# A hybrid decoder layer's third pass: TensorE's order by hand, p turned on TensorE, silu through tanh

## The chip, the core and the metric

The kernel runs on one core of a Trainium2 chip. The metric is the device time of one execution in microseconds, the median of several runs. The core has five engines that run beside each other and meet at semaphores: TensorE (PE in the profile, with PEld for its weight loads), VectorE (DVE), ScalarE (ACT), GpSimd (POOL) and SyncE (SP), which here issues the DMA transfers. Sixteen DMA engines move the data.

## The reference

One layer (depth 1, so only the gMLP mixer is built) on x of 4096 tokens by 1024, with a cross-attention of 4 heads of 64 into a memory of 256 rows. All in f32.

```python
kv = einsum('bmd,de->bme', mem, mem_kv_w)          # mem_k, mem_v: 4 heads x 64
proj = einsum('bsd,de->bse', x, a_w_in)
u, v, q_x, gate = split_cols(proj, [768, 768, 256, 1024])
tok = chunked_spatial_gating(u, v, a_w_s, a_b_s)    # gelu, norm per 128, causal 128 x 128 mixing, times u
s = einsum('bshd,bmhd->bhsm', qh, mem_k) * 64 ** -0.5
xo = einsum('bhsm,bmhd->bshd', softmax(s), mem_v)
mixed = concatenate([tok, xo], -1) * silu(gate)
y = einsum('bse,ed->bsd', mixed, w_out)
x = layer_norm(ALPHA * x + y, ln_g, ln_b)
```

## The kernel before

Each f32 operand of a product is kept as two parts of type fp32r, hi and lo (`split`, L70: a cast on ACT, then a subtraction on DVE), and a product is three matmuls for each 128 of depth (`product`, L187: 4 x 3 = 12 matmuls, each of 128 weights columns by the width of the output). The large products use seven partial products in place of eight (`x_parts`, `w_parts`, `gemm`), with the two halves of the 1024 columns of depth as one index.

The 4096 tokens are taken in 16 blocks of 256 (`b`), and the layer in four passes over all blocks, because not all weights fit. Passes 1 and 2 (L290) compute the two halves of u, v, the attention's q and the last 256 gate columns; they leave u times the mixed v (`z1_d`), q (`q_d`) and the gate columns for the attention (`gx_d`) in DRAM, and pass 2 leaves three of the four parts of x (`x_d`). `memory` (L245) makes K (`kst`) and V (`vst`) in pass 2.

Pass 3 (L393 to L507) is the one around the change. For each block it does the following:
- `load_x` (L406) brings the parts of x, `load_z` (L470) brings z1, one block's q comes in `scores`, gx in `attend`.
- `scores` (L417): for each half of the tokens (`c`) and pair of heads (`hp`), four matmuls into one PSUM bank (L426); maximum and scaling on DVE (L430, L431), two exps with their sums on ACT (L434), reciprocal on DVE, the product of p and 1/sum on POOL (L437). DVE then turns p within 32 x 32 squares into `pts` (L228, through `transposed`).
- `weights_of` (L441): sixteen DMA transfers on SP's queue (L447) put the turned squares in place in `pr`, and one split over 2048 columns makes `pT`.
- `attend` (L450): 16 matmuls of V by pT (L460), the adding of the two halves on ACT and DVE (L465, L466), the product with silu(gx) (L467), the store to `z_d`.
- the gates (L497): four quarters (column half `j`, token half `i`), each of two products, 24 matmuls of 384 columns (L190). ACT's Silu (L503), POOL's product with z1 (L505), DVE's turn into `zt`, and at the end of the block four transfers (`scatter`, L236).

`scores` runs two blocks and `weights_of` one block ahead of the gates in the text. The order on each engine is not that of the text: a planner simulates the engines and places each engine's instructions, DMA issues on SP's queue too. Pass 3 has eight PSUM banks: five for gates (`acc2`) and three for scores and attends (`oth2`).

Pass 4 (L510) multiplies z by w_out and does the norm. Two of its seven weights are loaded during pass 3 (L490), the other five (L514) go to places that hold pass 3's gate weights, V, K and `pT`. Its raw z tiles (`raw3`) use memory of pass 3's pools.

Of the kernel before, what the change touches and what calls it, by code (L numbers as in the profile page):

```python
# [13 lines left out]
P = 128  # L14
# [21 lines left out]
def trunk_kernel(ctx, tc, xT, x, memT, w_kv, wl, wsT, bsT, ln_g, ln_b, out):  # L36
# [11 lines left out]
    def f(ap):  # L48
        return ap.bitcast(F32)
# [195 lines left out]
    def memory(pool, psum):  # L245
# [32 lines left out]
        for mh in range(2):  # L278
            for h in range(HEADS):
                e = h % 2  # L280
                split(vst[:, mh, h, e * HD:(e + 1) * HD], vst[:, mh, h, (1 - e) * HD:(2 - e) * HD],
                      pv[:, mh, h * HD:(h + 1) * HD])
# [7 lines left out]
    for g in range(2):  # L290
        with tc.tile_pool(name=f"mix{g}", bufs=1, reuse_waits="tile") as pool, \
# [8 lines left out]
            if first:  # L300
# [6 lines left out]
                                    fill=0.0, base=0, channel_multiplier=-1)  # L307
            split(wm[:, 0], wm[:, 1], wraw)
# [84 lines left out]
    with tc.tile_pool(name="turned", bufs=1, reuse_waits="tile") as turned, \  # L393
            tc.tile_pool(name="att", bufs=1, reuse_waits="tile") as pool, \
            tc.tile_pool(name="acc2", bufs=5, space=bass.MemoryType.PSUM, reuse_waits="tile") as psum, \
            tc.tile_pool(name="oth2", bufs=3, space=bass.MemoryType.PSUM, reuse_waits="tile") as psum2:
# [4 lines left out]
        qss = [arena[:, o:o + 1024].rearrange("p (h t) -> p h t", h=HEADS) for o in (12288, 13312)]  # L401

# [14 lines left out]
        def scores(b):  # L417
            qs = qss[b % 2]
            nc.sync.dma_start(f(qs), q_d[b].rearrange("h p t -> p h t"))
            pts = turned.tile([P, 32, 2, 32], F32, name="pts")  # L420
            for c in range(2):
                for hp in range(2):
                    ps = oth("sc")
                    for e in range(2):
                        for i in range(2):
                            nc.tensor.matmul(ps[:, e, :], qs[:, 2 * hp + e, c * P:(c + 1) * P], kst[:, i, 2 * hp + e, :],  # L426
                                             start=i == 0, stop=i == 1)
                    nm = pool.tile([P, 2], F32, name="nm", bufs=2)
                    sm = pool.tile([P, 2], F32, name="sm", bufs=2)
                    nc.vector.tensor_reduce(nm, ps, axis=AX.X, op=ALU.max)  # L430
                    nc.vector.tensor_scalar(nm, nm, -SCALE, None, op0=ALU.mult)  # L431
# [51 lines left out]
        for b in range(NB):  # L483
            xs = nxt
            if b + 1 < NB:
                nxt = load_x(b + 1)
# [142 lines left out]
```

## Time and profile before

| what | value |
|---|---|
| median of 3 runs | 1580.45 us (1579.23 to 1582.13) |
| the profiled execution, its time | 1580.65 us |
| its span | 1578.8 us |
| mean granted TensorE clock | 0.948 |
| TensorE busy | 1386.1 us, 88% of the span |
| DVE, ACT, POOL busy | 1110.3, 793.5, 717.3 us |
| DMA | 322.65 MB, 204 GB/s on average |

The first 765 us or so are passes 1 and 2, the third pass runs to about 1208, the fourth to the end. The clock is a share of 2.4 GHz, and 0.5 is the lower level of 1.2 GHz. A window of the trace gives the busy time of each engine in a stretch, and the granted clock and the DMA engines' share beside it. Lines of the timeline merge instructions that follow each other and are of one kind; the bracket is the idle time ahead and what ended it. Busy time says little by itself: the waits and the order of the work in one stretch say what the stretch is worth.

### The profile page before, as it was taken

The numbers are of one execution on the slowest core, as the hardware profiler recorded it, in microseconds if no ns is written. First come the engines' busy times: TensorE is split into PE (matmuls) and PEld (weight loads), VectorE is DVE, ScalarE is ACT, GpSimd is POOL, SyncE is SP. The second block draws the span as 40 slices with busy tenths as digits, with TensorE's granted clock in tenths as the row PEclk, the third lists the DMA queues.
The fourth block names the chain that finished last, engine by engine and source line by source line (L and its number), as shares of the span: only waits on it lengthen the run. The fifth ranks groups of instructions, "written<-read, shape, count | busy, mean of one in ns | idle before, by whom it ended". The sixth has DMA issues, their size and how long they took to land.

```text
span 1578.8 us, 20546 instructions
## 1 busy us (share of the span) xinstructions
PE 1386.1 (88%) x6464; PEld 1162.3 (74%) x6464; DVE 1110.3 (70%) x2043; ACT 793.5 (50%) x1535; POOL 717.3 (45%) x530
## 2 busy tenths in 40 slices
PE   2799999999999999999699989898934989888987
PEld 1577877777777878788698989888933767766775
DVE  5887788778578877777445555656542888888887
ACT  4465555545445554455367767677842422322231
POOL 4644543343344345443133332323232776667674
PEclk9899999999999999999799989999966999999999
DMA  6477678566998595858988888878788545455443
GB/s 199 139 204 199 167 211 209 154 151 196 363 278 274 191 302 180 270 170 261 369 215 235 216 217 222 219 207 243 170 269 270 135 135 159 140 141 150 131 121 93
DMA packets 382957, 322.65 MB, mean 204 GB/s; under 512 B 216704, under 2 KB 344960, under 8 KB 380544
## 3 DMA queue, kind: packets, MB, share of 16 engines
q1 hardware_dynamic: 382848, 321.34, 70.3%
q8 instruction: 51, 0.84, 0.2%
q14 instruction: 58, 0.48, 0.1%
HBM read 183.38 MB, written 121.11 MB: 193 GB/s over the span
## 4 chain that ended last, share of the span: by engine, by line
DMA 25%; PE 20%; DVE 19%; SPq 10%; issue 9%; ACT 9%; POOL 7%; POOLq 0%; DVEq 0%; ACTq 0%
PE accw L190 8%; DVE xc L72 7%; PE accx L190 5%; PE accq L190 5%; SPq L447 5%; DMA raw<-xT 3%; DMA x<-xT 3%; DMA xc<-xd 2%; DMA xr<-x 2%; ACT vg L377 2%; ACT xc L71 2%; DMA wd<-xc 2%; DMA arena<-wd 2%; SPq L240 2%; DMA z1d<-u 2%
## 5 line engine op out<-in xcount | busy, mean ns | idle before, releaser
L190 PE MATMUL accw<-arena,xc 128*128 128x512 f32 x1728 | 453.0, 409 | 67.1 <-ACT xc L71 39.4
L190 PEld LDWEIGHTS accw<-arena,xc 128*128 128x128 f32 x1728 | 331.8, 195 | 155.9 <-ACT xc L71 41.8
L190 PE MATMUL accx<-arena,xc 128*128 128x512 f32 x1152 | 304.5, 406 | 22.4 <-ACT arena L71 12.4
L190 PE MATMUL accq<-arena,xc 128*128 128x512 f32 x1152 | 293.0, 396 | 2.4 <-ACT cs L574 2.0
L190 PE MATMUL gate<-arena,xc 128*128 128x384 f32 x1536 | 285.6, 342 | 0.0
L190 PEld LDWEIGHTS accx<-arena,xc 128*128 128x128 f32 x1152 | 220.2, 193 | 78.3 <-ACT arena L71 12.8
L190 PEld LDWEIGHTS gate<-arena,xc 128*128 128x128 f32 x1536 | 270.0, 193 | 0.0
L72 DVE TENSOR_TENSOR xc<-sums,xc 128x512 fp32r<-128x512 f32 x224 | 188.8, 848 | 102.3 <-ACT xc L71 101.7
L190 PEld LDWEIGHTS accq<-arena,xc 128*128 128x128 f32 x1152 | 214.6, 188 | 52.8 <-ACT cs L574 2.4
L71 ACT CAST xc<-sums 128x512 fp32r<-128x512 f32 x224 | 135.6, 616 | 169.6 <-POOL sums L81 79.5
L72 DVE TENSOR_TENSOR xc<-raw,xc 128x512 fp32r<-128x512 f32 x180 | 159.5, 887 | 23.7 <-ACT xc L71 23.6
L437 POOL TENSOR_TENSOR sums<-sums,sm 128x512 f32<-128x512 f32 x64 | 66.6, 1040 | 229.8 <-DVE sm L436 215.0
L80 POOL TENSOR_TENSOR sums<-raw 128x512 f32<-128x512 f32 x48 | 66.7, 1391 | 165.7 <-DMA raw<-xT 103.3
L71 ACT CAST xc<-raw 128x512 fp32r<-128x512 f32 x180 | 110.6, 616 | 40.0 <-PE accq L190 15.2
L533 ACT ACTIVATE xr<-xr 128x1024 f32<-128x1024 f32 x32 | 33.9, 1060 | 177.9 <-DMA xr<-x 156.2
L377 ACT ACTIVATE vg<-vg,nm,rs 128x128 f32<-128x128 f32 x192 | 77.9, 483 | 89.8 <-DVE nm L374 89.8
L88 POOL TENSOR_TENSOR sums<-raw,sums 128x512 f32<-128x512 f32 x48 | 74.0, 1541 | 99.2 <-DVE xc L72 90.9
L373 POOL TENSOR_TENSOR rs<-rs,mhalf 128x6 f32<-128x6 f32 x32 | 49.8, 1557 | 89.0 <-DVE rs L372 88.2
L505 POOL TENSOR_TENSOR z<-z,cs 128x384 f32<-128x384 f32 x64 | 64.0, 1023 | 51.5 <-DMA z<-z1d 34.6
L228 DVE STREAM_TRANSPOSE pts<-sums 128x512 f32<-128x512 f32 x64 | 41.8, 689 | 61.7 <-DMA pr<-pts 49.4
L460 PE MATMUL at<-arena 128*128 128x256 f32 x256 | 43.2, 320 | 41.7 <-ACT arena L71 38.6
L426 PE MATMUL sc<-arena 128*128 128x256 f32 x256 | 47.0, 321 | 35.6 <-ACT sums L434 32.2
(101 smaller groups left out, 1934.1 us busy)
## 6 DMA issues: line engine op xcount, KB each, us to landing
raw<-xT SPq DMA_DIRECT2D x64, 512.0 KB, 5.2
wd<-xc SPq DMA_DIRECT2D x56, 512.0 KB, 5.0
arena<-wd SPq DMA_DIRECT2D x14, 2048.0 KB, 12.8
xd<-xc SPq DMA_DIRECT2D x48, 512.0 KB, 3.5
xc<-xd SPq DMA_DIRECT2D x48, 512.0 KB, 8.1
raw<-wl SPq DMA_DIRECT2D x38, 512.0 KB, 4.0
pr<-pts SPq DMA_DIRECT2D x256, 64.0 KB, 2.2
raw<-zd SPq DMA_DIRECT2D x32, 512.0 KB, 4.4
```

The lines of the kernel that those rows point to most:

```text
L71: nc.scalar.copy(hi, src)
L72: nc.vector.tensor_tensor(lo, src, f(hi), op=ALU.subtract)
L80: tt(s1, a21, a22, op=ALU.add)
L88: tt(s4, a12, s2, op=ALU.subtract)
L190: nc.tensor.matmul(acc, t[:, a, k, :], w[:, b, k, :], start=first and k == 0 and i == 0, stop=last and k == KH - 1 and i == 2, skip_group_ ...
L373: nc.gpsimd.tensor_tensor(rs, rs, mhalf.rearrange("p (h c) -> p h c", c=2), op=ALU.pow)
L377: nc.scalar.activation(vg[:, h, c, :], vg[:, h, c, :], AF.Identity, bias=nm[:, h, c:c + 1], scale=rs[:, h, c:c + 1])
L426: nc.tensor.matmul(ps[:, e, :], qs[:, 2 * hp + e, c * P:(c + 1) * P], kst[:, i, 2 * hp + e, :], start=i == 0, stop=i == 1)
L437: nc.gpsimd.tensor_tensor(p, p, sm.unsqueeze(2).broadcast_to([P, 2, M]), op=ALU.mult)
L447: nc.sync.dma_start(dst[j * 32:(j + 1) * 32, :, q, :], src[q * 32:(q + 1) * 32, :, j, :])
L460: nc.tensor.matmul(ps[:, e, :], vst[:, mh, h, :], pT[:, a, 2 * h + mh, :], start=i == 0, stop=i == 3)
L505: nc.gpsimd.tensor_tensor(z, z, gate, op=ALU.mult)
```

## The change

p is no longer turned by DVE and sixteen transfers: TensorE turns it, four 128x128 transposes in f32 per `turn` into a PSUM bank, and two strided operations (cast on ACT, subtraction on DVE) write it to `pT` in the same order of tokens. Silu becomes (1 + tanh(g/2)) g with tanh on ACT and the rest in one operation on DVE; the factor 1/2 goes into V, the spatial weights and their bias. `attend` runs for block b - 1 at the head of block b, `scores` and `turn` come in pieces between the quarters of the gates, and within pass 3 TensorE's order is that of the text (`manual_schedule` for PE); the other engines' orders are still the planner's. PSUM is now three banks for gates and five for the rest; the pool `turned` is gone, and p has tiles of its own.

```diff
--- before.py
+++ after.py
@@ -278,8 +278,10 @@
         for mh in range(2):
             for h in range(HEADS):
                 e = h % 2
-                split(vst[:, mh, h, e * HD:(e + 1) * HD], vst[:, mh, h, (1 - e) * HD:(2 - e) * HD],
-                      pv[:, mh, h * HD:(h + 1) * HD])
+                hi, lo = vst[:, mh, h, e * HD:(e + 1) * HD], vst[:, mh, h, (1 - e) * HD:(2 - e) * HD]
+                v = pv[:, mh, h * HD:(h + 1) * HD]
+                nc.scalar.mul(hi, v, 0.5)
+                nc.vector.scalar_tensor_tensor(lo, v, 0.5, f(hi), op0=ALU.mult, op1=ALU.subtract)
         for t, d in zip(kst, k_d):
             nc.sync.dma_start(d, f(t))
         nc.sync.dma_start(v_d, f(vst))
@@ -305,6 +307,9 @@
             nc.sync.dma_start(wraw, wsT[:, 3 * g:3 * g + 3, :])
             nc.gpsimd.affine_select(out=wraw, in_=wraw, pattern=[[0, 3], [1, P]], compare_op=ALU.is_ge,
                                     fill=0.0, base=0, channel_multiplier=-1)
+
+            nc.scalar.mul(wraw, wraw, 0.5)
+            nc.scalar.mul(bs, bs, 0.5)
             split(wm[:, 0], wm[:, 1], wraw)
 
             for b in range(NB):
@@ -390,15 +395,19 @@
     both.close()
 
 
-    with tc.tile_pool(name="turned", bufs=1, reuse_waits="tile") as turned, \
-            tc.tile_pool(name="att", bufs=1, reuse_waits="tile") as pool, \
-            tc.tile_pool(name="acc2", bufs=5, space=bass.MemoryType.PSUM, reuse_waits="tile") as psum, \
-            tc.tile_pool(name="oth2", bufs=3, space=bass.MemoryType.PSUM, reuse_waits="tile") as psum2:
+    with tc.tile_pool(name="att", bufs=1, reuse_waits="tile") as pool, \
+            tc.tile_pool(name="acc2", bufs=3, space=bass.MemoryType.PSUM, reuse_waits="tile") as psum, \
+            tc.tile_pool(name="oth2", bufs=5, space=bass.MemoryType.PSUM, reuse_waits="tile") as psum2:
         wg = [[view(o, GW) for o in r] for r in ((24576, 28672), (0, 3072))]
         vst = arena[:, 27648:28672].rearrange("p (a h d) -> p a h d", a=2, h=HEADS)
         kst = arena[:, 6144:8192].rearrange("p (a h m) -> p a h m", a=2, h=HEADS)
         pT = arena[:, 8192:12288].rearrange("p (a j t) -> p a j t", a=2, j=2 * HEADS)
         qss = [arena[:, o:o + 1024].rearrange("p (h t) -> p h t", h=HEADS) for o in (12288, 13312)]
+
+        ident = pool.tile([P, P], F32, name="ident")
+        nc.vector.memset(ident, 1.0)
+        nc.gpsimd.affine_select(out=ident, in_=ident, pattern=[[1, P]], compare_op=ALU.is_equal, fill=0.0, base=0,
+                                channel_multiplier=-1)
 
         def oth(name):
             return psum2.tile([P, 2, TB], F32, name=name, tag="oth")
@@ -414,43 +423,45 @@
             split(a21[:, 0], a21[:, 1], raw)
             return (a11, a12), (a21, a22)
 
-        def scores(b):
-            qs = qss[b % 2]
-            nc.sync.dma_start(f(qs), q_d[b].rearrange("h p t -> p h t"))
-            pts = turned.tile([P, 32, 2, 32], F32, name="pts")
-            for c in range(2):
-                for hp in range(2):
-                    ps = oth("sc")
-                    for e in range(2):
-                        for i in range(2):
-                            nc.tensor.matmul(ps[:, e, :], qs[:, 2 * hp + e, c * P:(c + 1) * P], kst[:, i, 2 * hp + e, :],
-                                             start=i == 0, stop=i == 1)
-                    nm = pool.tile([P, 2], F32, name="nm", bufs=2)
-                    sm = pool.tile([P, 2], F32, name="sm", bufs=2)
-                    nc.vector.tensor_reduce(nm, ps, axis=AX.X, op=ALU.max)
-                    nc.vector.tensor_scalar(nm, nm, -SCALE, None, op0=ALU.mult)
-                    p = sum_tile().rearrange("p k c -> p (k c)").rearrange("p (h m) -> p h m", h=2)
-                    for e in range(2):
-                        nc.scalar.activation(p[:, e, :], ps[:, e, :], AF.Exp, bias=nm[:, e:e + 1], scale=SCALE,
-                                             accum_out=sm[:, e:e + 1])
-                    nc.vector.reciprocal(sm, sm)
-                    nc.gpsimd.tensor_tensor(p, p, sm.unsqueeze(2).broadcast_to([P, 2, M]), op=ALU.mult)
-                    transposed(pts[:, 16 * hp:16 * hp + 16], p.rearrange("p h m -> p (h m)"), c)
-            return pts
-
-        def weights_of(pts):
-            raw = turned.tile([P, 2 * HEADS, TB], F32, name="pr")
-            dst = raw.rearrange("p k (q s) -> p k q s", q=4)
-            src = pts.rearrange("p (k j) c t -> p k j (c t)", j=4)
-            for q in range(4):
-                for j in range(4):
-                    nc.sync.dma_start(dst[j * 32:(j + 1) * 32, :, q, :], src[q * 32:(q + 1) * 32, :, j, :])
-            split(pT[:, 0], pT[:, 1], raw)
-
-        def attend(b):
+        def load_q(b):
+            nc.sync.dma_start(f(qss[b % 2]), q_d[b].rearrange("h p t -> p h t"))
+
+        def scores(b, c, hp):
+
+            ps = oth("sc")
+            for e in range(2):
+                for i in range(2):
+                    nc.tensor.matmul(ps[:, e, :], qss[b % 2][:, 2 * hp + e, c * P:(c + 1) * P],
+                                     kst[:, i, 2 * hp + e, :], start=i == 0, stop=i == 1)
+            nm = pool.tile([P, 2], F32, name="nm", bufs=4)
+            sm = pool.tile([P, 2], F32, name="sm", bufs=4)
+            nc.vector.tensor_reduce(nm, ps, axis=AX.X, op=ALU.max)
+            nc.vector.tensor_scalar(nm, nm, -SCALE, None, op0=ALU.mult)
+            p = pool.tile([P, 2, M], F32, name="p", bufs=4)
+            for e in range(2):
+                nc.scalar.activation(p[:, e, :], ps[:, e, :], AF.Exp, bias=nm[:, e:e + 1], scale=SCALE,
+                                     accum_out=sm[:, e:e + 1])
+            nc.vector.reciprocal(sm, sm)
+            nc.gpsimd.tensor_tensor(p, p, sm.unsqueeze(2).broadcast_to([P, 2, M]), op=ALU.mult)
+            return p
+
+        def turn(p, c, hp):
+            pt = psum2.tile([P, 4, P], F32, name="pt", tag="oth")
+            for i in range(4):
+                nc.tensor.transpose(pt[:, i, :], p[:, i // 2, i % 2 * P:(i % 2 + 1) * P], ident)
+            hi, lo = (pT[:, a, 4 * hp:4 * hp + 4, :].rearrange("p k (q c t) -> p k q c t", q=4, c=2)[:, :, :, c, :]
+                      for a in range(2))
+            split(hi, lo, pt.rearrange("p k (q t) -> p k q t", q=4))
+
+        def load_gx(b):
             gx = pool.tile([P, 2, TB], F32, name="gx", bufs=2)
             nc.sync.dma_start(gx, gx_d[b].rearrange("k p t -> p k t"))
-            nc.scalar.activation(gx, gx, AF.Silu)
+            th = cs_tile().rearrange("p (k t) -> p k t", k=2)
+            nc.scalar.activation(th, gx, AF.Tanh, scale=0.5)
+            nc.vector.scalar_tensor_tensor(gx, th, 1.0, gx, op0=ALU.add, op1=ALU.mult)
+            return gx
+
+        def attend(b, gx):
             zx = pool.tile([P, 2, TB], F32, name="zx")
             for hp in range(2):
                 ps = oth("at")
@@ -478,33 +489,52 @@
         for i in range(2):
             nc.sync.dma_start(f(kst[:, i]), k_d[i])
         nc.sync.dma_start(f(vst), v_d)
-        weights_of(scores(0))
-        pts = scores(1)
-        for b in range(NB):
-            xs = nxt
-            if b + 1 < NB:
-                nxt = load_x(b + 1)
-            z1s = [load_z(b, j) for j in range(2)]
-            attend(b)
-            if b in (4, 8):
-                weights(3, (b // 8,))
-            if b + 1 < NB:
-                weights_of(pts)
-            if b + 2 < NB:
-                pts = scores(b + 2)
-            zt = pool.tile([P, 24, 2, 32], F32, name="zt")
-
-            for j in range(2):
-                for i in range(2):
-                    acc = psum.tile([P, 512], F32, name="gate", tag="acc")[:, :GW]
-                    for h in range(2):
-                        product(acc, xs[i][h], wg[j][h], h == 0, h == 1)
-                    gate = cs_tile()[:, :GW]
-                    nc.scalar.activation(gate, acc, AF.Silu)
-                    z = z1s[j][:, i]
-                    nc.gpsimd.tensor_tensor(z, z, gate, op=ALU.mult)
-                    transposed(zt[:, 12 * j:12 * j + 12], z, i)
-            scatter(z_d[b][:NH], zt)
+        load_q(0)
+        gx = None
+        with tc.manual_schedule(engines={mybir.EngineType.PE}):
+            for b in range(NB):
+                xs = nxt
+                z1s = [load_z(b, j) for j in range(2)]
+                zt = pool.tile([P, 24, 2, 32], F32, name="zt")
+                accs = {}
+
+                def gate(i, j, h):
+                    if h == 0:
+                        accs[i, j] = psum.tile([P, 512], F32, name="gate", tag="acc")[:, :GW]
+                    acc = accs[i, j]
+                    product(acc, xs[i][h], wg[j][h], h == 0, h == 1)
+                    if h == 1:
+                        g = cs_tile()[:, :GW]
+                        nc.scalar.activation(g, acc, AF.Tanh, scale=0.5)
+                        nc.vector.scalar_tensor_tensor(g, g, 1.0, acc, op0=ALU.add, op1=ALU.mult)
+                        z = z1s[j][:, i]
+                        nc.gpsimd.tensor_tensor(z, z, g, op=ALU.mult)
+                        transposed(zt[:, 12 * j:12 * j + 12], z, i)
+
+                if b:
+                    attend(b - 1, gx)
+                p0, p1 = scores(b, 0, 0), scores(b, 1, 0)
+                gx = load_gx(b)
+                if b + 1 < NB:
+                    nxt = load_x(b + 1)
+                    load_q(b + 1)
+                gate(0, 0, 0)
+                gate(0, 0, 1)
+                p2, p3 = scores(b, 0, 1), scores(b, 1, 1)
+                gate(1, 0, 0)
+                turn(p0, 0, 0)
+                gate(1, 0, 1)
+                turn(p1, 1, 0)
+                gate(0, 1, 0)
+                gate(0, 1, 1)
+                turn(p2, 0, 1)
+                gate(1, 1, 0)
+                turn(p3, 1, 1)
+                gate(1, 1, 1)
+                scatter(z_d[b][:NH], zt)
+                if b in (4, 8):
+                    weights(3, (b // 8,))
+            attend(NB - 1, gx)
 
 
     with tc.tile_pool(name="raw3", bufs=1, reuse_waits="tile") as raw3, \
```

## Rows read from the trace of the kernel before

**Rows 1.** Windows: length, busy of PE, PEld, DVE, ACT, POOL, clock, DMA share, GB/s.

```profile
765.00:1210.00 445.00, 357.24 (x2038) 342.84 (x2039) 234.35 (x439) 292.82 (x539) 134.35 (x131) 0.89 0.84 228
...
765.00:800.00 35.00, 22.48 (x113) 21.58 (x114) 14.61 (x34) 19.83 (x47) 9.59 (x9) 0.71 0.99 332
800.00:1120.00 320.00, 291.75 (x1697) 281.77 (x1696) 177.26 (x332) 228.88 (x410) 99.62 (x99) 0.96 0.82 215
...
1150.00:1210.00 60.00, 15.49 (x63) 13.14 (x62) 25.03 (x43) 22.04 (x43) 15.29 (x15) 0.58 0.82 248
```

**Rows 2.** Timeline of SP's queue: start us, us, line, transfer, how many.

```profile
1021.65 0.59 SPq L412 DMA_DIRECT2D x<-xT  x1
1022.34 12.05 SPq L447 DMA_DIRECT2D pr<-pts  x10
...
1047.48 0.65 SPq L412 DMA_DIRECT2D x<-xT  x1
```

**Rows 3.** Timeline of PE: start us, us, line, operation, how many.

```profile
748.30 2.96 PE L190 MATMUL accx<-arena,xc 128*128 128x512 f32 x12
...
793.19 16.13 PE L190 MATMUL gate<-arena,xc 128*128 128x384 f32 x92
...
1147.06 1.83 PE L460 MATMUL at<-arena 128*128 128x256 f32 x14
1148.73 3.64 PE L190 MATMUL gate<-arena,xc 128*128 128x384 f32 x20
```

**Rows 4.** Groups of 765 to 1210: operation, shapes, count, busy us, mean ns, idle before.

```profile
L437 POOL TENSOR_TENSOR sums<-sums,sm 128x512 f32<-128x512 f32 x64 | 66.6, 1040 | 229.8 <-DVE sm L436 215.0 <-DVE nm L431 14.6
L434 ACT ACT_TABLE_LOAD x47 | 60.3, 1283 | 34.2 <-DVE nm L431 31.0 <-PE gate L190 2.8
L430 DVE TENSOR_REDUCE nm<-sc 128x2 f32<-128x512 f32 x64 | 43.1, 677 | 6.5 <-DMA z1d<-u 5.6 <-PE sc L426 0.5
L228 DVE STREAM_TRANSPOSE pts<-sums 128x512 f32<-128x512 f32 x64 | 41.8, 689 | 61.7 <-DMA pr<-pts 49.4 <-POOL sums L437 12.3
L72 DVE TENSOR_TENSOR arena<-pr,arena 128x2048 fp32r<-128x2048 f32 x16 | 36.6, 2288 | 19.1 <-ACT arena L71 19.0
...
L431 DVE TENSOR_SCALAR nm<-nm 128x2 f32<-128x2 f32 x64 | 20.2, 329 | 0.8
L72 DVE TENSOR_TENSOR xc<-x,xc 128x512 fp32r<-128x512 f32 x16 | 15.6, 976 | 4.4 <-ACT xc L71 4.4
...
L71 ACT CAST xc<-x 128x512 fp32r<-128x512 f32 x16 | 9.7, 616 | 1.6 <-PE gate L190 1.6
...
L386 DVE SCALAR_TENSOR_TENSOR u<-mixed,bs,u 128x256 f32<-128x256 f32 x3 | 1.4, 484 | 1.6 <-PE mixed L384 1.6
```

**Rows 5.** Timeline of PE at the pass's end; the bracket is idle time before.

```profile
1197.04 0.80 PE L460 MATMUL at<-arena 128*128 128x256 f32 x2 [24.04 <-ACT arena L71]
1199.36 3.36 PE L460 MATMUL at<-arena 128*128 128x256 f32 x14 [1.53 <-DVE arena L72]
1207.97 1.22 PE L190 MATMUL accw<-arena,xc 128*128 128x512 f32 x2 [5.25 <-ACT xc L71]
```

**Rows 6.** Windows with weight loads (first) and p transfers (second) on the DMA engines.

```profile
1175.00:1182.00 7.00, 0.00 (x0) 0.00 (x0) 3.02 (x6) 1.72 (x4) 1.11 (x2) 0.61 1.00 424
...
1188.50:1194.00 5.50, 0.00 (x0) 0.00 (x0) 0.00 (x0) 0.00 (x0) 0.00 (x0) 0.50 0.63 134
```

**Rows 7.** A piece of the chain of waits: start us, us, what.

```profile
1069.78 1.02 ACT sums L434 x4
```

**Rows 8.** The start: a piece of the chain of waits, then PE's timeline.

```profile
762.76 16.55 DMA z1d<-u
...
785.13 4.84 PE L190 MATMUL gate<-arena,xc 128*128 128x384 f32 x21
```

**Rows 9.** The handover: SP's timeline, then a window of the products (L190) alone.

```profile
1199.34 0.38 SPq L112 DMA_DIRECT2D raw<-zd  x1
...
1205.00:1230.00 25.00, 20.90 (x76) 16.12 (x77) 0.82 0.93 319
```

## The prediction

> **What bounds the kernel now.** I read the busy time of the third pass first, as windows. From 765 to 1210 us TensorE is busy 357 of 445 us, at a granted clock of 0.89. It loses time in three places: at the start (765 to 800), a little all along (800 to 1120: 292 of 320, clock 0.96), and most at the end (1150 to 1210: 15.5 of 60, clock 0.58) [rows 1].
>
> What sets the pace in the middle? The load of the next block's x leaves SP's queue at 1021.65 and again at 1047.48, so a block takes 25.8 us [rows 2]. Its TensorE work is less. 92 gate matmuls run in 16.13 us; less 0.34 for the last one that is 0.1735 us each. 14 attend matmuls start 1.67 us ahead of what follows them, 0.12 each, and the scores have the same shape [rows 3]. A block is 96 x 0.1735 + 32 x 0.12 = 16.66 + 3.84 = 20.5 us. So TensorE is not the bound; a loop through other engines is. SP issues 16 small transfers per block, ten of which take 12.05 us of its queue in one stretch [rows 2]. ACT must then cast the turned p before attend, and between exps and silu it changes tables: 47 loads of 1.283 us ahead of exps [rows 4], and about as many back, some 120 of the 293 us that ACT is busy [rows 1].
>
> Gates don't wait for this loop but attends do, so TensorE runs out of gates at 1152.4 [rows 3] with two attends left. The last of them follows 24.04 us of idle, until ACT has cast p, and the fourth pass begins only at 1207.97 [rows 5].
>
> **The change, removals.** (a) The 256 p transfers, 16 issues per block off SP. While these hold the DMA engines almost alone, eight of them cost a share of 0.63 over 5.5 us [rows 6], 3.5 us, so 16 cost 6.9 us of a block's 0.82 x 25.8 = 21.2. The 14.3 that remain lie below any period forecast here. (b) The table loads, if exp and tanh share a table; no row shows a tanh, so both cases are priced. (c) DVE's turn of p (41.8 us busy) and its long subtraction (16 x 2.288) with the long cast ahead of it [rows 4].
>
> **Additions.** ACT: 64 casts of 128x512, by the like cast at 0.616 us, 39 us; tanh for silu at the same size. Even without credit for the long casts ACT falls to 293 - 120 + 39 = 212 us, 13.3 per block. DVE: 64 gate products of 128x384 from PSUM. The same operation at 128x256 took 0.484, a 128x512 subtraction 0.976; I take 0.62 between them, 40 us. Also 64 subtractions from PSUM and 16 gx products at up to 0.976, 78 us; less 42 + 37 us [rows 4]. DVE goes from 234 to about 273 us, 17.1 per block. POOL keeps its products, 134 us, 8.4 per block [rows 1]. All of this lies beside TensorE as long as its block is longer than 17.1 us; without that cover DVE's +39 us would be paid. The halvings of v, of the spatial weights and of the bias are a handful of small operations beside streaming matmuls of earlier passes, and the identity is made once: nothing, or some 2 us if on the path.
>
> TensorE gets 256 transposes of 128x128 in plain f32, which no row shows. From below: 512 columns go every 0.233 us (2.96 less 0.40 for the last, by 11), 384 every 0.1735, 256 every 0.12 [rows 3], so about 0.06 per 128 columns. From above: if plain f32 takes four passes, 4 x 0.065 = 0.26. I take 0.12, the row nearest in columns, since each also loads its own 128 weights: 16 x 0.12 = 1.9 us per block. A block is then 20.5 + 1.9 = **22.4 us**, and TensorE becomes the bound.
>
> The Trainium skill, TensorE: Matmul & The Clock Gate, Part 4: PE-mode transpose, speaks against this: it gives about 275 ns for a transpose in a kernel, and says that the full clock doesn't engage for this mode. By its price the sum would be 256 x 0.155 = 40 us higher, an estimate of about 1570.
>
> **The new waits.** TensorE's order is now fixed, so a turn that waits for its p holds every gate behind it. The chain from scores to p is 0.68 (maximum) + 0.33 (scaling) [rows 4] + 1.02 (two exps with their sums, a piece of the chain of waits) [rows 7] + 0.33 at most (reciprocal of the same small shape) + 1.04 (POOL) [rows 4] = 3.4 us; I add 2 for queueing behind attend's copies and adds. Between p0's scores and its turn the order puts other scores and 36 gates: 0.5 + 6.2 + 1.0 = 7.7 us; for p2 it is over 8. The last turn has 12 gates and half an attend, 2.1 + 1.0 = 3.1 us, ahead of the matmuls that need it, against a cast and a subtraction of 0.6 + 1.0 plus hand-offs: the thinnest cover. All fit, so I allow 0.5 us of stall per block (bounds 0 and 1.5). The loads of x, q, gx and z that move on SP's queue lose the 16 issues they stood behind; the scatter's four still wait there for the last gate product, ahead of the next block's loads. Each is needed half a block or more later, so I cost this at nothing; with a cover lost it would be a DMA landing, some 5 to 8 us once.
>
> **The sum**, on the profiled run (span 1578.8, its time 1580.65; the median of the three is 1580.45, the same within 0.02%). Start: 24 gates ran at 760, the next at 785.13, while the store of the pass before took 16.55 us to land [rows 8] at a DMA share of 0.99 [rows 1]. The change leaves that traffic, so I keep the point: block 0 has 72 gates and 16 transposes left, 12.5 + 1.9, and ends at 799.5. Then 15 x 22.4 = 336.0, at 1135.5; stalls 16 x 0.5 = 8, at 1143.5; the last attend 1.9, at 1145.4. Handover: before, the second z load of the fourth pass could go at 1199.34, and 76 of its products were done by 1230 [rows 9], which at 0.233 is full rate since 1212.3: 13.0 us. With 1 more for the last z product the fourth pass counts from 1159.4. Four of its five late weight loads, 2 MB each, now start only when gates and attend end. At the 424 GB/s of 1175 to 1182 [rows 6] they take 20 us, with z's 2 MB 25, so they land until 1171; the last is needed at 1159.4 + 6 x 2.8 = 1176. I add 2 us for the earlier ones: 1161.4 in place of 1212.3. The rest of the fourth pass runs as before. Gain 50.9 us; 1580.65 - 50.9 = 1529.8, say **1530**.
>
> **Rivals.** (1) Transposes take four passes: 256 x 0.14 = +36 us, **1566**. For it, the plain f32 type; against it, nothing in the trace. 0.12. (2) Tables still alternate, now between exp and tanh: 8 loads of 1.283 put ACT at 13.3 + 10.3 = 23.6 us per block, longer than TensorE's, and p comes late. With 2.5 us per block, **1570**. 0.05. The Trainium skill, ScalarE: Activation LUTs, Table sets, lists tanh in the set of exp; no run so far shows it. (3) The fixed order starves: ACT or DVE take their queues in another order than I did, and turns wait. Each us per block is 16 us; 2.5 more gives **1570**. 0.12, a third of it beyond break-even, which is 50.9 / 16 = 3.2 us per block. (4) **Slower:** the clock stays down. After the long wait the last 14 attend matmuls took 3.36 us in place of 1.83 [rows 3, 5]; at the lower level, 1.2 GHz, a block costs up to 20 us more. If short turns and stalls bring it down, break-even is 50.9 / 20 = 2.5 of 16 blocks, and five low blocks give **1630**. For it, 0.58 at the idle end; against it, 0.96 in a middle that idles a tenth of the time already [rows 1], more than is forecast. 0.05. The sentence of the Trainium skill above is this rule; no transpose in this trace tests it. (5) The middle stays held by DMA landings, 24 to 25 us per block: **1565**. Against it, the 14.3 us of DMA left. 0.06.
>
> **How the numbers follow.** The forecast has 0.60. Its low end: transposes at 0.065 (-14), no stalls (-8), a handover 3 us shorter: 1505. The high end takes in rivals 1, 2, 3 and 5: 1572. About 0.2% is what a measurement here can tell from no change. Slower 0.04 + 0.05 = 0.09; same, a rival near break-even, 0.03; faster 0.88.
>
> **What would show it.** Right: no table loads between exps and tanhs, one attend per 22 to 23 us, a granted clock near 1.00, turns of about 0.5 us between gates, and some 12 us of little work before the fourth pass. Wrong: turns waiting for POOL's product, over 0.2 us per transpose, a clock under 0.9 in the middle, or the fourth pass's first products waiting for weights.

## The result, and the profile after

The changed kernel takes 1550.26 us (1549.91 to 1553.85, three runs) against 1580.45: a ratio of 0.9823 [0.9804, 0.9841]. That is 30 us less, where the prediction said 51 and gave 1505 to 1572. Its profiled execution took 1549.91 us, with a span of 1548.2; the gain on the profiled runs, which the sum was made for, is 30.74 us.

The windows of the third pass come first: length, busy time of PE, PEld, DVE, ACT and POOL with their instructions, granted clock, DMA share, GB/s. They answer [rows 1].

```profile
755.00:800.00 45.00, 30.64 (x146) 27.46 (x145) 18.81 (x50) 15.09 (x38) 8.32 (x8) 0.81 1.00 370
800.00:1120.00 320.00, 320.00 (x2066) 317.85 (x2065) 202.32 (x441) 147.92 (x425) 122.40 (x114) 1.00 0.70 193
1120.00:1145.00 25.00, 23.59 (x155) 23.24 (x153) 15.49 (x35) 11.30 (x33) 9.59 (x9) 1.00 0.63 180
1145.00:1177.00 32.00, 0.00 (x0) 0.00 (x0) 1.43 (x3) 0.41 (x1) 2.97 (x3) 0.53 1.00 356
```

The middle is now TensorE's: 320 of 320 us busy at a clock of 1.00 (291.75 and 0.96 before), while no other engine reaches two thirds. Right behind it stands a hole: 32 us without a single matmul, in which nearly nothing runs but the DMA engines, at a share of 1.00. The missing 20 us are mainly there.

TensorE's timeline (start, us, line, operation, how many, and in brackets the idle time ahead and what ended it) shows the start, one block, the end of the pass and the first product of the next. It answers [rows 3, 5].

```profile
789.82 4.29 PE L190 MATMUL gate<-arena,xc 128*128 128x384 f32 x12 [6.64 <-ACT xc L71]
...
806.71 2.08 PE L471 MATMUL at<-arena 128*128 128x256 f32 x16
808.63 1.12 PE L434 MATMUL sc<-arena 128*128 128x256 f32 x8
809.59 4.33 PE L190 MATMUL gate<-arena,xc 128*128 128x384 f32 x24
...
816.82 0.60 PE L451 MATMUL pt<-ident,p 128*128 128x128 f32 x4
817.17 2.34 PE L190 MATMUL gate<-arena,xc 128*128 128x384 f32 x12
819.35 0.60 PE L451 MATMUL pt<-ident,p 128*128 128x128 f32 x4
...
829.03 2.08 PE L471 MATMUL at<-arena 128*128 128x256 f32 x16
...
1141.51 2.08 PE L471 MATMUL at<-arena 128*128 128x256 f32 x16
1177.26 1.22 PE L190 MATMUL accw<-arena,xc 128*128 128x512 f32 x2 [33.67 <-ACT xc L71]
```

Attend to attend is 829.03 - 806.71 = 22.32 us, and the fifteen blocks from 806.71 to 1141.51 take 334.8, the same 22.32 each. No line between carries a bracket. Over 780 to 1150 the view of TensorE's waits has a single one:

```profile
PE gate L190 <- ACT xc L71: 6.6, 1, 6.6
```

The groups of 765 to 1210 (operation, shapes, count; busy us, mean ns of one; idle time before and its cause) hold the added work, in the place of [rows 4].

```profile
L72 DVE TENSOR_TENSOR arena<-pt,arena 128x512 fp32r<-128x512 f32 x64 | 44.1, 689 | 6.6 <-ACT arena L71 6.2
L451 PE MATMUL pt<-ident,p 128*128 128x128 f32 x256 | 38.7, 274 | 0.0
L71 ACT CAST arena<-pt 128x512 fp32r<-128x512 f32 x64 | 37.7, 590 | 3.9 <-PE pt L451 3.9
L509 DVE SCALAR_TENSOR_TENSOR cs<-cs,gate 128x384 f32<-128x384 f32 x64 | 35.3, 551 | 57.0 <-ACT cs L508 55.8
L442 ACT ACT_TABLE_LOAD x1 | 1.3, 1283 | 0.0
```

From 765 to 1210 one table load is left of the 47 ahead of exps. The cast is at 0.590 us (0.616 taken), the gate product at 0.551 (0.62 taken), the subtraction at 0.689 (0.976 at most).

Last the handover, from SP's queue (the loads answer [rows 9]). The view merges the five weight loads into one line; the first three lines here are from narrower windows, which part them.

```profile
1129.49 0.34 SPq L184 DMA_DIRECT2D arena<-wd  x1
1141.18 0.84 SPq L184 DMA_DIRECT2D arena<-wd  x2
1143.62 0.80 SPq L184 DMA_DIRECT2D arena<-wd  x2
1144.96 19.36 SPq L240 DMA_DIRECT2D zd<-zt  x4
1164.42 0.57 SPq L479 DMA_DIRECT2D zd<-zx  x1
1165.03 0.74 SPq L111 DMA_DIRECT2D raw<-zd  x1
1167.43 0.36 SPq L112 DMA_DIRECT2D raw<-zd  x1
```

Of the five late weight loads of the fourth pass, 2 MB each, the first went out 15 us ahead of the last block's four stores of z. The other four, 8 MB, were issued from 1141.18 to 1144.42, right ahead of these stores. The stores took 19.36 us only to issue, the last of them landed at 1167.29 (a piece of the chain of waits: 5.89 us from 1161.40), and z can be read back only then. So the second z load goes at 1167.43 and the first product runs at 1177.26. Of the products alone (L190), the window from 1145 to 1230 is:

```profile
1145.00:1230.00 85.00, 48.95 (x194) 38.69 (x195) 0.78 0.70 219
```

With 194 products by 1230, at the 0.233 us of the prediction, this is full rate since 1230 - 45.2 = 1184.8. The forecast was 1161.4; before, it was 1212.3 [rows 9].

### The profile page after: what moved, and what is told of

Its sections match the earlier page's. It is cut to its first block, busy times and chain, and to the rows that moved or that the text cites. A ratio compares the mean times of both kernels' runs of the same rounds, so it can differ in the third digit from the quotient of the medians.

```text
span 1548.2 us, 20794 instructions
## 1 busy us (share of the span) xinstructions
PE 1394.0 (90%) x6720; PEld 1179.7 (76%) x6720; DVE 1119.0 (72%) x2108; ACT 675.8 (44%) x1493; POOL 727.8 (47%) x531
## 4 chain that ended last, share of the span: by engine, by line
PE 39%; DVE 21%; DMA 17%; issue 8%; ACT 6%; SPq 5%; POOL 3%; DVEq 0%; POOLq 0%; ACTq 0%
PE gate L190 17%; DVE xc L72 7%; PE accw L190 6%; PE accq L190 4%; PE accx L190 4%; DMA xr<-x 4%; DMA wd<-xc 3%; ACT vg L382 3%; DVE xr L587 2%; ACT xc L71 2%; PE sc L434 2%; PE at L471 2%; DMA out<-xr 2%; DMA raw<-xT 2%; PE pt L451 2%
## 5 line engine op out<-in xcount | busy, mean ns | idle before, releaser
L190 PE MATMUL accw<-arena,xc 128*128 128x512 f32 x1728 | 456.6, 411 | 97.4 <-ACT xc L71 67.6
L190 PEld LDWEIGHTS accw<-arena,xc 128*128 128x128 f32 x1728 | 333.8, 196 | 186.5 <-ACT xc L71 69.7
L190 PE MATMUL accx<-arena,xc 128*128 128x512 f32 x1152 | 302.7, 404 | 19.7 <-ACT arena L71 12.7
L190 PE MATMUL accq<-arena,xc 128*128 128x512 f32 x1152 | 294.0, 397 | 4.5 <-ACT cs L212 3.1
L190 PE MATMUL gate<-arena,xc 128*128 128x384 f32 x1536 | 290.9, 342 | 6.6 <-ACT xc L71 6.6
L190 PEld LDWEIGHTS accx<-arena,xc 128*128 128x128 f32 x1152 | 219.6, 193 | 75.2 <-ACT arena L71 13.2
L190 PEld LDWEIGHTS gate<-arena,xc 128*128 128x128 f32 x1536 | 265.2, 190 | 7.1 <-ACT xc L71 6.8
L190 PEld LDWEIGHTS accq<-arena,xc 128*128 128x128 f32 x1152 | 215.1, 189 | 55.5 <-ACT cs L212 4.1
L72 DVE TENSOR_TENSOR xc<-raw,xc 128x512 fp32r<-128x512 f32 x180 | 163.0, 906 | 25.4 <-ACT xc L71 25.3
L80 POOL TENSOR_TENSOR sums<-raw 128x512 f32<-128x512 f32 x48 | 67.5, 1406 | 167.3 <-DMA raw<-xT 90.3
L511 POOL TENSOR_TENSOR z<-z,cs 128x384 f32<-128x384 f32 x64 | 72.1, 1127 | 139.3 <-DVE cs L509 73.8
L445 POOL TENSOR_TENSOR p<-p,sm 128x512 f32<-128x512 f32 x64 | 65.3, 1042 | 90.0 <-DVE sm L444 80.6
L442 ACT ACTIVATE p<-sc,nm 128x256 f32<-128x256 f32 x128 | 59.0, 474 | 67.3 <-DVE nm L439 67.3
L509 DVE SCALAR_TENSOR_TENSOR cs<-cs,gate 128x384 f32<-128x384 f32 x64 | 35.3, 551 | 57.0 <-ACT cs L508 55.8
L85 POOL TENSOR_TENSOR sums<-raw 128x512 f32<-128x512 f32 x48 | 67.0, 1396 | 17.8 <-DVE xc L72 17.8
```

The lines of the kernel that those rows point to most:

```text
L72: nc.vector.tensor_tensor(lo, src, f(hi), op=ALU.subtract)
L80: tt(s1, a21, a22, op=ALU.add)
L85: tt(s3, a11, a21, op=ALU.subtract)
L190: nc.tensor.matmul(acc, t[:, a, k, :], w[:, b, k, :], start=first and k == 0 and i == 0, stop=last and k == KH - 1 and i == 2, skip_group_ ...
L442: nc.scalar.activation(p[:, e, :], ps[:, e, :], AF.Exp, bias=nm[:, e:e + 1], scale=SCALE, accum_out=sm[:, e:e + 1])
L445: nc.gpsimd.tensor_tensor(p, p, sm.unsqueeze(2).broadcast_to([P, 2, M]), op=ALU.mult)
```

## Experiments

Each kernel's ratio is against the kernel before, run beside it on the same chip. The changed kernel, run a second time so, gave 1550.5 us, 0.9816 [0.9786, 0.9845], which is the yardstick for the others.

> The changed kernel as it is, on the chip of the three kernels below, so that they are compared on one chip: 1547 to 1553.

### Which part of the change brings the gain

**The turn alone.** Everything of the change but tanh (and its halvings) and the hand-written order:

```diff
...
-            nc.scalar.activation(th, gx, AF.Tanh, scale=0.5)
-            nc.vector.scalar_tensor_tensor(gx, th, 1.0, gx, op0=ALU.add, op1=ALU.mult)
+            nc.scalar.activation(gx, gx, AF.Silu)
...
-        with tc.manual_schedule(engines={mybir.EngineType.PE}):
+        if True:
...
-                        nc.scalar.activation(g, acc, AF.Tanh, scale=0.5)
-                        nc.vector.scalar_tensor_tensor(g, g, 1.0, acc, op0=ALU.add, op1=ALU.mult)
+                        nc.scalar.activation(g, acc, AF.Silu)
```

> The changed kernel without the silu through tanh (and the halvings) and without the order by hand: of the change only the turn on TensorE, attend one block behind in the text, and the new split of the banks. Since the change without tanh alone gave 1545 and without the order by hand alone 1548, theory G says that the turn on TensorE is the whole gain: 1543 to 1552. Rival: tanh and the order each cover for the other (with Silu ACT is later, and only a fixed order or only short ACT work hides it): 1560 or more.

Measured: 1546.53 us, 0.9788 [0.9759, 0.9817]. Its middle, and the table loads that it still makes (windows, then groups):

```profile
800.00:1120.00 320.00, 320.00 (x2070) 317.89 (x2069) 167.74 (x374) 222.37 (x482) 115.58 (x114) 1.00 0.68 191
```

```profile
L437 ACT ACT_TABLE_LOAD x31 | 39.8, 1283 | 7.8 <-DVE nm L434 7.8
L501 ACT ACT_TABLE_LOAD x17 | 21.8, 1283 | 0.3
L454 ACT ACT_TABLE_LOAD x15 | 19.2, 1283 | 0.3
```

ACT still makes 63 loads, 81 us, and is busy 222 of 320; TensorE is as full as in the whole change. What is left of the change is the whole gain: the turn, and what came with it (the attend one block later, the scores in pieces, p's own tiles, the new split of the banks), which no run takes apart. For short it is called the turn below.

**Silu back** (the first and last hunk above, and no halvings), TensorE's order kept by hand:

> The changed kernel with Silu in place of tanh and of the gates' operation on DVE, without the halvings of V, the spatial weights and the bias. Theory D, the tables don't matter once p is turned on TensorE: ACT is busy some 10 us of a 22.3 us block, 4 to 8 loads of 1.283 us bring it to 15 to 20, TensorE stays the bound: +8 us or less, 1548 to 1558. Rival: the loads lie in the chain from scores to turn and hold TensorE there: a block of 24 us or more, +30 us, 1580.

Measured: 1544.88 us, 0.9775 [0.9745, 0.9804]. Tanh brings nothing; if anything it costs a few us.

**TensorE's order left to the planner** (the middle hunk alone):

> The changed kernel with TensorE's order in the third pass left to the planner. Theory E, the order by hand keeps TensorE full: the planner puts turns and scores where their inputs are late, TensorE waits 1 to 2 us per block and loses clock, +15 to 40 us, 1565 to 1590. Rival: with the p transfers and the table loads gone any order does: within 5 us of 1550.

Measured: 1548.33 us, 0.9808 [0.9775, 0.9841], the same as with the order by hand. The planner's order also keeps TensorE busy 320 of 320 us from 800 to 1120. So the hand-written order has no part in the gain, and the theory that gave it one fell.

**Tanh alone** (with its halvings), in the kernel before:

```diff
...
-            nc.scalar.activation(gx, gx, AF.Silu)
+            th = cs_tile().rearrange("p (k t) -> p k t", k=2)
+            nc.scalar.activation(th, gx, AF.Tanh, scale=0.5)
+            nc.vector.scalar_tensor_tensor(gx, th, 1.0, gx, op0=ALU.add, op1=ALU.mult)
...
-                    nc.scalar.activation(gate, acc, AF.Silu)
+                    nc.scalar.activation(gate, acc, AF.Tanh, scale=0.5)
+                    nc.vector.scalar_tensor_tensor(gate, gate, 1.0, acc, op0=ALU.add, op1=ALU.mult)
```

> The kernel before with silu through tanh (and the halvings) as the only edit. Theory F: the loop of p transfers, long cast and exps holds the block at 25.8 us, and the loads of tables are only part of it; the loads vanish, a block gets 1 to 2 us shorter, the idle end stays at about 50 us: 1555 to 1570. Rival: SP's queue and the DMA engines alone hold the loop, 1575 to 1583. If the tables were the whole cause, a block of 22 us and 1530 or less.

Measured: 1588.13 us, 1.0053 [1.0031, 1.0076], slower. TensorE's waits from 800 to 1170 (engine, what waited, for what: us, times, longest) say why nothing was won. First those of the kernel before, then those of this one:

```profile
PE sc L426 <- ACT sums L434: 24.9, 20, 2.2
PE at L460 <- ACT arena L71: 14.6, 5, 9.1
```

```profile
PE gate L190 <- DVE cs L511: 24.2, 10, 4.4
PE at L467 <- ACT arena L71: 11.5, 6, 2.7
...
PE sc L431 <- ACT sums L439: 1.6, 2, 1.3
```

The table loads did hold TensorE up, as far as waits can show it: its scores waited 24.9 us for ACT's exps. Without the loads that wait shrinks to 1.6 us, and another of the same size takes its place. Silu freed the gates' PSUM bank on ACT; now the added operation on DVE frees it, and DVE still makes the turns of p and the long subtraction. So in that kernel the wait moved from ACT to DVE. The 8 us that it lost are not in these waits, which come to 41.3 us in all against 44.2, and where they lie stays open. The loads' cost was real and could not be had by this means; with the turn gone from DVE, ACT and SP, the two forms of silu come out within a few us of each other.

### What a turn costs

```diff
-            for i in range(4):
+            for i in (0, 1, 2, 3) * 2:
```

Each transpose is done twice into the same place.

> The changed kernel with each of the 256 transposes issued twice into the same place. Theory C, TensorE is the bound of the middle and a transpose costs what its spacing in the trace shows (four in 0.35 us, 0.089 each): +23 us, about 1573, a block 1.4 us longer. If a transpose really costs 0.275 us, as the price that spoke against the change: +70 us, 1620, and a lower granted clock. If TensorE has slack in the middle: no change.

Measured: 1573.45 us, 0.9961 [0.9947, 0.9974], 23 us more for 256 transposes. On TensorE's timeline, one block and the last attend:

```profile
806.98 2.08 PE L471 MATMUL at<-arena 128*128 128x256 f32 x16
...
817.08 1.03 PE L451 MATMUL pt<-ident,p 128*128 128x128 f32 x8
817.87 2.34 PE L190 MATMUL gate<-arena,xc 128*128 128x384 f32 x12
...
831.06 2.08 PE L471 MATMUL at<-arena 128*128 128x256 f32 x16
...
1168.17 2.08 PE L471 MATMUL at<-arena 128*128 128x256 f32 x16
```

A block takes 24.08 us, 1.76 more, so a transpose costs 0.11 us; the middle grows by 361.2 - 334.8 = 26.4. (I had expected 23 from the 0.35 us between the start of a turn of four and that of the gates behind it, 0.089 each. The total hit that figure, but the four added ones cost more than the first four: a turn of eight starts 0.79 us ahead of the gates, 0.44 more, which is 0.11 each. On the profiled runs, the whole is 1575.87 against 1549.91 and 1554.01, between 22 and 26.) Two things follow. A price of 0.275 us, 70 us for the 256, is out. And what TensorE got more to do in the middle was paid in full: nothing else bounds it.

### The start: two early weight loads

Two of the fourth pass's weights are loaded during the third. The planner had placed both at its very start, ahead of pass 2's last stores of the gate columns. Here each stands behind the store of block 4 or 8:

```diff
-            nc.sync.dma_start(dv[q], src[q * 32:(q + 1) * 32].rearrange("i j c t -> i j (c t)"))
+            last[:] = [nc.sync.dma_start(dv[q], src[q * 32:(q + 1) * 32].rearrange("i j c t -> i j (c t)"))]
...
-                    weights(3, (b // 8,))
+                    with tc.issue_after(last[0].ins):
+                        weights(3, (b // 8,))
```

> The changed kernel, with the two weight loads (2 MB each) that the planner moved ahead of the second pass's last stores put back behind the scatters of blocks 4 and 8 on SP's queue. Theory B: these 4 MB hold the stores, and behind them the x load that block 0's second quarter waits for (6.6 us idle of TensorE at 789.8, and the lower clock around it). Then block 0 ends 10 to 15 us earlier than at 806.7, and the time is about 1537. Rival: the start is held by the last norm chain of the second pass and by the x load itself; 3 us or less, 1547 to 1550.

Measured: 1541.51 us, 0.9748 [0.9721, 0.9774]. SP's queue at the start, first in the changed kernel, then here:

```profile
762.28 4.90 SPq L184 DMA_DIRECT2D arena<-wd  x2
767.29 0.52 SPq L393 DMA_DIRECT2D z1d<-u  x1
767.91 11.96 SPq L240 DMA_DIRECT2D gxd<-gt  x4
```

```profile
764.30 4.11 SPq L241 DMA_DIRECT2D gxd<-gt  x4
```

The stores issue in 4.11 us in place of 11.96, the first attend runs at 795.19 in place of 806.71, and the whole gains some 9 us. The kernel before has the same placing (the two loads issue at 757.59, the stores behind them take 11.88 us), so this gain isn't one of the change.

### The handover

**The weights behind the first z loads.** Four of the five late weights are issued after the last block's stores and the first two loads of z:

```diff
-        nc.sync.dma_start(r1, src1)
+        last[:] = [nc.sync.dma_start(r1, src1)]
...
-        ws = weights(3, range(2, 7))
         nxt = parts_of(z_d[0].rearrange("k p t -> p k t"), x_parts)
+        ws = weights(3, (3,))
+        with tc.issue_after(last[0].ins):
+            weights(3, (2, 4, 5, 6))
```

> The changed kernel, with four of the fourth pass's five late weight loads (2, 4, 5 and 6, 8 MB) placed on SP's queue behind the last block's scatter and the first two z loads. Theory A, the queue: TensorE stood idle for 33.7 us after the last attend because the scatter and the z loads were queued behind 10 MB of weights. Then the first product of the fourth pass comes near 1162 us in place of 1177, the weights land until about 1177, just behind the products that need them, and the time falls by 15 to 25 us, to about 1530. Rival, the bytes: the pass needs the same 10 MB whatever their order, so products start earlier but wait for weights; 5 us or less, 1545 to 1550.

Measured: 1543.59 us, 0.9764 [0.9736, 0.9792]: some 7 us, where 15 to 25 were expected. TensorE's timeline, then ACT's:

```profile
1159.01 1.22 PE L191 MATMUL accw<-arena,xc 128*128 128x512 f32 x2 [17.93 <-ACT xc L72]
...
1183.63 4.95 PE L191 MATMUL accq<-arena,xc 128*128 128x512 f32 x12 [10.94 <-ACT cs L607]
```

```profile
1182.05 1.06 ACT L566 ACTIVATE xr<-xr 128x1024 f32<-128x1024 f32 x1 [14.28 <-DMA xr<-x]
1183.01 0.57 ACT L607 COPY cs<-accq 128x512 f32<-128x512 f32 x1
```

(The 10 MB of the expectation count the load that went out first; 8 MB were issued right ahead of the stores.) The stores issue in 3.16 us, and the first product runs 18 us earlier, at 1159.01. But then TensorE stops again. It waits for a PSUM bank that ACT must copy, and ACT, in order, stands at the scaling of the block's x, whose load is queued behind 8 MB of weights.

**The same with p's buffers first in memory**, so that z's raw tile doesn't wait for the tile that the last stores read:

> As h_order, and the tiles of p are given the first places of the third pass's memory, so that the second raw z tile of the fourth pass no longer lies on zt and need not wait for the last scatter to land. Theory A with the memory as a second link: the second z load goes 4 to 6 us earlier, the first product comes near 1158, and the time is 3 to 5 us under h_order. If the order on the queue alone was the cause: the same as h_order within 2 us.

Measured: 1542.91 us, 0.9757 [0.9726, 0.9788], first product at 1158.93, stop of 12.07 at 1183.81. The memory link is worth nothing.

**The weights, and the norm's two vectors, also behind block 0's eight loads of x**, with p's buffers first as well. Shown is the part of the edit in the loop over blocks of the fourth pass:

```diff
...
+            if b == 0:
+                with tc.issue_after(last[0].ins):
+                    weights(3, (2, 4, 5, 6))
+                    nc.sync.dma_start(lg, ln_g.partition_broadcast(P))
+                    nc.sync.dma_start(lb, ln_b.partition_broadcast(P))
```

> As h_both, and the four weight loads also stand behind block 0's eight loads of x (1 MB) for the fourth pass, with the norm's two vectors behind the weights. In h_order and h_both the products began at 1159 instead of 1177 but then stopped for 11 to 12 us behind a copy on ACT. Theory H: ACT stood at its scaling of x, in order, until the x load came in behind 8 MB of weights; with x ahead of them that stop shrinks to 3 us or less, and the time is 8 to 10 us under h_both, about 1534. Rival, the bytes: the weights come 2.5 us later and the products wait for them instead: within 3 us of h_both's 1543.

Measured: 1543.94 us, 0.9773 [0.974, 0.9807]. The stop at 1183 is gone, and one of the same length stands 11 us later, for the next block's x (TensorE, ACT, then the windows of the changed kernel and of this one):

```profile
1194.62 1.22 PE L191 MATMUL accw<-arena,xc 128*128 128x512 f32 x2 [10.34 <-ACT xc L72]
```

```profile
1191.23 1.06 ACT L565 ACTIVATE xr<-xr 128x1024 f32<-128x1024 f32 x1 [21.01 <-DMA xr<-x]
```

```profile
1150.00:1190.00 40.00, 12.74 (x48) 10.14 (x48) 5.88 (x7) 7.28 (x11) 6.36 (x5) 0.61 0.96 302
```

```profile
1150.00:1190.00 40.00, 22.46 (x84) 16.74 (x84) 16.51 (x23) 6.81 (x11) 10.72 (x9) 0.80 1.01 344
```

By order, then, the stop moves and keeps its size. Put on one scale (end of the last attend; products by 1230, from one window of L190 or L191, 1145 to 1230; the point since which that is full rate, at 0.233 us each):

| kernel | attend ends | products | full rate since | between |
|---|---|---|---|---|
| changed | 1143.6 | 194 | 1184.8 | 41.2 |
| weights behind z | 1141.1 | 218 | 1179.2 | 38.1 |
| and p's buffers first | 1142.4 | 218 | 1179.2 | 36.8 |
| weights also behind x | 1142.2 | 224 | 1177.8 | 35.6 |

From 1150 to 1190 the DMA share is 0.96 to 1.01 in all four, at 302 to 353 GB/s, 12.1 to 14.1 MB. The order is worth 3 to 6 us of the 41.2; the rest goes by with DMA engines busy for 0.91 to 0.96 of it in every order. Busy isn't fast, though: with the weights behind z the engines move 179 GB/s at a share of 0.81 from 1143 to 1152, when the stores and z go, and 412 at 1.00 from 1153 to 1177, when the weights do.

**Both starts and ends mended.** The early weights moved, with the handover of the third kernel of the table, and with that of the fourth:

> h_both and i_start together. If A and B each hold and lie at different ends of the third pass, their gains add: about 1515. If one of them only moves its wait elsewhere, the sum is the other's alone, 1525 to 1537.

> k_xr and i_start together. By theories B and H the gains add: 1523 to 1528. By the rival of k_xr: the 1535 of j_all.

Measured: 1534.96 us, 0.9716 [0.9685, 0.9747], and 1535.49, 0.9715 [0.9688, 0.9742]. The two gains add up (9 and 7), the two handovers end level again, and both kernels beat the changed one by 15 us and the kernel before by 44. Their last attends end at 1134.8 and 1135.7, their full rate counts from 1172.2 and 1171.3: 37.4 and 35.6 between.

## Why the prediction was right in direction and 20 us short

**The start: 7 us off.** The forecast let block 0 end at 799.5; its attend runs at 806.71. The gates came back at 789.82, where the prediction kept 785.13: 4.7 us. The other 2.5 are the clock: behind the stop of 6.64 the first twelve gates take 4.29 us, against 2.34 at full speed, and no low clock was summed there. "The change leaves that traffic" was right, and the traffic itself, two weight loads ahead of stores that others wait for, stood in the rows only as a DMA share of 0.99. Moving it gave 11.5 us.

**The middle: right, 9 us to the good.** TensorE became the bound, as forecast, at 22.32 us per block against 22.4. The transposes cost 0.11 each where 0.12 was taken. The 8 us for stalls were not needed: every cover named held, the thinnest too. So the middle took 334.8 in place of 344.0, and the attend that follows it starts 2 us before the forecast in spite of the late start. By the estimate from the Trainium skill, TensorE: Matmul & The Clock Gate, Part 4: PE-mode transpose, it would have been 40 us more. The trace has the page's duration, 274 ns as the mean of one such instruction, but they overlap and cost 0.11 each. It differs on the clock: the granted clock is 1.00 throughout in the windows of the middle.

**The removals: the right sum by a partly wrong reading.** I named two things that hold the loop, transfers and table loads. Tables alone, taken away, brought no gain, as their wait moved to DVE. With the turn moved, leaving them in cost nothing. That the set of exp serves tanh too, as the Trainium skill, ScalarE: Activation LUTs, Table sets, has it, the trace confirms: one load in the pass. The fixed order, which two rivals feared, neither cost nor gained.

What holds the loop of the kernel before is settled only so far: taking the turn out takes the transfers, DVE's turns, the long cast and the long subtraction out at once, and I didn't part these, nor the new split of the banks and the attend's later place.

**The handover: the step that failed.** 16 us were summed from the end of the last attend to the fourth pass, 41.2 passed. "Four of its five late weight loads now start only when gates and attend end" held: they were issued from 1141.18 to 1144.42. What failed is what the sum made of it. It took the 13.0 us of the kernel before from the second z load to full rate, and "I add 2 us for the earlier ones" priced a queue as if z went first; but the planner had put the four ahead of the last stores and of z. The wrong sign that I listed last, products waiting for weights, came in another form: z itself waited behind the weights. The Trainium skill, DMA: Bandwidth & Descriptors, Queues, rings and completion order, says that each DMA engine consumes descriptors in the order of its ring; the four stores agree, the last landing 22.3 us after the first was issued behind 8 MB.

But order is the smaller part. With z first, the first product runs at 1159.01, near the 1159.4 from which the prediction, but for those 2 us, counted full rate; full rate itself counts only from 1179.2. The sum had counted four weights and 2 MB of z, 25 us at 424 GB/s. By the groups of DMA issues (eight x loads of 128 KB and two z loads of 512 KB per block) these 2 MB are the z of two blocks. Left out were two blocks' x (2 MB), the last stores (four of 192 KB and one of 256 KB, 1 MB) and the norm's two vectors (1 MB), and the rate is 302 to 353 GB/s with these among them. All that is 14 times 1.049 MB, 14.7; at 350 GB/s that is an estimate of 42 us. The trace has 14.24 MB from 1141 to 1186.

The row that should have told it stood in [rows 1]: the end of the old pass moved 248 GB/s x 60 us = 14.9 MB. I read that stretch as TensorE waiting for p, which the waits support, and took it as free to go. It was also time in which weights moved, as SP's queue of the kernel before shows:

```profile
1145.22 0.42 SPq L184 DMA_DIRECT2D arena<-wd  x1
...
1169.91 0.89 SPq L184 DMA_DIRECT2D arena<-wd  x2
...
1202.75 0.81 SPq L184 DMA_DIRECT2D arena<-wd  x2
```

Three of the five late loads, 6 MB, went out before or during the wait for p, and only two were left behind z's first loads (the second at 1199.34). The 13.0 us are the price of that handover. With the wait gone the cover is gone too: one load is out before the last attend, and 8 MB are left. So of the 60 us from gates' end to full rate (1152.4 to 1212.3), 43 stayed (1141.7 to 1184.8) and 17 went.

That bytes set this bound is argued, not shown: four orders of the same loads support it, which end within 6 us of each other on DMA engines that are busy nearly throughout. A rival is left. In three of the four TensorE's long stop hangs on ACT, which stands in order at its scaling of x; with that scaling placed behind the copies and casts that TensorE waits for, the stop might go though the bytes stay. Neither that nor a kernel with fewer bytes there, or with the weights in memory earlier, was tried, so how much of the 36 us could be hidden stays open.

**The account**, on the profiled runs: start +7.2, middle -9.2, so the attend ends 1.8 before the forecast 1145.4. Handover +25.2: full rate at 1184.8 in place of 1161.4, 23.4 late. The rest of the fourth pass 3.2 shorter. Together 20.2, the difference between 50.9 and 30.7.

## What to carry to other kernels

A stretch in which the bounding engine idles has more than one thing in it: before you count it as gained, add up what the DMA engines move there and divide by the rate that they reach; here more than half of the stretch stayed. Where a planner or a compiler places transfers, take their order from the queue's own rows of a trace and not from the text, and ask of every large load what small store is issued behind it. And when a change joins several edits, run each alone: here one of three, with what came along with it, brought everything, and one of them alone made the kernel slower.

## What the runs showed of the hardware

- 128x128 transposes of f32 on TensorE cost 0.11 us each when added between other matmuls (24.08 less 22.32, by 16), though one of them is recorded at 274 ns.
- They didn't lower the clock: 1.00 from 800 to 1120 with 16 of them per block, and with 32.
- Four stores of 192 KB, issued right behind four loads of 2 MB, held SP's queue for 19.36 us, against 3.16 with one load some 15 us ahead of them. So large loads just ahead delayed not only the landing but the issue of what followed.
- A table load is 1.283 us, but 63 of them in the pass cost nothing where ACT, loads included, is busy 222 of 320 us and TensorE is the bound.
